# Value projections of the second and third attention group: from two products to one block of 1024 columns by Strassen's method

## The chip, the cores and the metric

The kernel runs on one core of a Trainium2 chip. The metric is the device time of one launch in microseconds. Three runs of the kernel before gave 2731.43 to 2731.93 us, with a median of 2731.71 us; the same kernel with the change is to be timed against it.

## What is computed

Two layers of a post-norm encoder on 256 tokens of 2048 features, all in float32. In each layer `x @ w_in` gives the queries, keys and values of two attentions and two gates; the first attention ("dilated") has three head groups, the second is a windowed attention with grouped queries. Cut to what the change touches:

```python
proj = jnp.einsum('bsd,dc->bsc', x, w_in)              # x: 256 x 2048
qa, ka, va, qb, kb, vb, ga, gb = jnp.split(proj, split_points, axis=-1)
ya = dilated_mixture(qa, ka, va, rel_bias).astype(dt) @ w_pa     # va: 3 groups x 512 columns
yb = windowed_gqa(qb, kb, vb, rel_bias, sink).astype(dt) @ w_pb
merged = jax.nn.sigmoid(ga) * ya + jax.nn.sigmoid(gb) * yb
x = layer_norm(DEEPNORM_ALPHA * x + merged @ w_out, ln1_g, ln1_b)
gate, up = jnp.split(x @ w_up, 2, axis=-1)
x = layer_norm(DEEPNORM_ALPHA * x + (jax.nn.silu(gate) * up) @ w_down, ln2_g, ln2_b)
```

## The kernel before

**Products in three parts.** Every float32 operand of a large product is split into a high part (rounded to the matmul's short float format) and the rest: `split_into` (lines 468 to 470) writes `hi` on ScalarE (ACT) and `lo = src - hi` on VectorE (DVE). A product of two operands is then three matmuls into one PSUM bank: high times high, high times low, low times high (`rows_product`, lines 242 to 247).

**Pieces.** The program is a list of pieces. A piece is one 512 KB weight tile (two tiles of 128 rows by 512 columns, or four by 256) with its load, its split and its matmuls. `run` (line 166) walks the list: before the matmuls of piece m it issues the splits up to piece m + 5 (further ahead round a layer norm, by the `norms` list), and `load_to` issues the loads up to five pieces beyond the split, into seven `raw` buffers on SP's DMA queue. After the matmuls of a piece comes its `post`, and then one entry of the list `soon` or, if that is empty, of `background` (attention steps, bias tables, the affine step of the layer norm), unless the piece is marked `quiet`. What is issued later in this order stands later in the in-order queue of each engine.

**Two ways to do 1024 columns.** `gemm_a` (line 249) multiplies all 256 tokens by 512 columns over 16 tiles of the contraction: 8 pieces, 96 matmuls of 128 x 512, one accumulator (`acc`, two PSUM banks, two buffers). `gemm_s` (line 306) does two such column blocks c1 and c2 together. The 16 contraction tiles are eight pairs. In three of them, marked S in the plan `SCSCSCCC`, it forms seven products instead of eight, so 21 matmuls instead of 24; the other five, C, are done plainly. An S pair takes four pieces (`pair_of_sums`, line 342): the first two load the left and right weight tile, and the four splits of them do on DVE: one full split and the half-width ones `t13`, `b22` (lines 354 to 356), three half-width sums (lines 365 to 368), and two full splits of the sums, `thi` and `tlo`. Its pieces are quiet, as are the C pairs between S pairs. The products of an S pair collect in four single banks (`aux`: q1, q5, q7, q6) and in the four banks of both accumulators (q2, q3 in the first, q4 and the last in the second); the last S pair folds the single banks into two tiles e and f, and the last C pair adds e and f to the accumulators. In three of the C pairs (list `ADDED`) the left tile is split by ACT and a POOL DMA instead of DVE. Before an S pair can run, `sum_rows` (line 439) must have formed the sums of the tokens' side for its pair: four DVE additions, an ACT copy and a DVE subtraction, `sT`.

**The start of a layer.** Here each layer computes the values of the first attention by three `gemm_a` (lines 861 to 863, called VA0, VA1, VA2 below), then the values of the second attention (VB, line 864, 4 pieces), its keys (KB) and its queries. `post_va` (line 834) brings the result to SBUF: for group 0 as a split pair on ACT and DVE, for the others as plain float32, one half on ACT and one on DVE. Pieces are numbered from 0 at the layer's first. In layer 0 the first six pieces also transpose the input (`make`, each with a split `xT` on ACT and DVE), and piece 6 queues the small tables (`setup_small`): the background then holds `turn`, `biases` (a product with the table `hots`) and seven writes of the table `ftab` on SP. In layer 1 the first pieces of VA0 are interleaved with the layer norm before it, and piece 4 adds `late` and twelve background entries of the affine step.

**Where gemm_s is used already.** The gates of column blocks 1 to 3 (`both`, line 916, after one plain `gate(0)`), and 10 of the 11 column blocks of the up product. The first `both` of a layer is called both(1) below; its three `sum_rows` run in the pieces just before it.

## Time and profile before

| | |
|---|---|
| runs, us | 2731.43, 2731.71, 2731.93 |
| profiled execution, us | 2733.02 (span 2731.2) |
| mean granted TensorE clock | 0.997 |
| busy us: TensorE (PE) / weight loads / DVE / ACT / POOL | 2701.2 / 2269.0 / 1894.5 / 1382.3 / 72.8 |
| matmuls / DVE / ACT instructions | 13209 / 2354 / 1679 |
| DMA: MB, mean GB/s | 572.77, 210 |

The span runs from the first to the last instruction; the profiled execution's time is 1.8 us more. A matmul's record in the timeline has a start and a modelled length; neighbouring records overlap, so the distance between starts is what a matmul costs. Three things tell about a place of the program: the start times on PE, the idle time in brackets with what ended it, and what DVE and ACT did at that time.

### The profile page before, as it was taken

What the parts mean: (1) busy time and instruction counts of PE and PEld (TensorE: products, weight loads), DVE (VectorE), ACT (ScalarE), POOL (GpSimd) and SP (SyncE); (2) the same over time, 40 slices, a digit from 0 to 9 for tenths busy, and PEclk for the clock granted to TensorE, in tenths of its full rate; (3) what the DMA queues carried; (4) which work ended last, traced back from release to release, by engine and by line L of the source; (5) the groups of instructions that cost most, each with busy time, mean ns of one, the idle gap of its engine ahead of it and who ended that gap; (6) DMA issues with size and microseconds to landing.
All of it is one profiled execution on the core that took longest, in us unless ns stands there. A gap on an engine that the chain in (4) does not pass through costs nothing. (4 is left out here: it accounts for less than half of the span.)

```text
span 2731.2 us, 35220 instructions
## 1 busy us (share of the span) xinstructions
PE 2701.2 (99%) x13209; PEld 2269.0 (83%) x13209; DVE 1894.5 (69%) x2354; ACT 1382.3 (51%) x1679; POOL 72.8 (3%) x91
## 2 busy tenths in 40 slices
PE   9999999999999999999999999999999999999998
PEld 7888878888888888888888888788888788888887
DVE  5566577766985687577675655777678857875885
ACT  4454455544564465455454544555455545553551
POOL 0000000000000000000000000000000000000000
PEclk9999999999999999999999999999999999999999
DMA  8866567764886687578566565677648757875874
GB/s 260 255 183 182 185 180 241 219 211 139 242 264 208 193 242 232 198 213 255 202 198 180 180 189 174 213 208 231 224 131 249 244 197 206 245 239 177 246 224 132
DMA packets 368991, 572.77 MB, mean 210 GB/s; under 512 B 53536, under 2 KB 150816, under 8 KB 368820
## 3 DMA queue, kind: packets, MB, share of 16 engines
q1 hardware_dynamic: 356788, 528.31, 58.9%
q0 software_dynamic: 11232, 40.90, 8.1%
q8 instruction: 103, 1.69, 0.3%
q10 hardware_dynamic: 800, 1.31, 0.1%
q14 instruction: 68, 0.56, 0.1%
HBM read 522.86 MB, written 6.68 MB: 194 GB/s over the span
## 5 line engine op out<-in xcount | busy, mean ns | idle before, releaser
L470 DVE TENSOR_TENSOR wlo<-raw,whi 128x1024 fp32r<-128x1024 f32 x804 | 951.2, 1220 | 199.0 <-ACT whi L469 155.3
L469 ACT ACTIVATE whi<-raw 128x1024 fp32r<-128x1024 f32 x804 | 815.4, 1052 | 275.3 <-PE acc L247 132.4
L329 PE MATMUL acc<-whi,xT 128*128 128x512 f32 x1118 | 440.3, 394 | 2.9 <-DVE sg L414 2.9
L331 PE MATMUL acc<-whi,xT 128*128 128x512 f32 x1118 | 435.9, 390 | 0.0
L330 PE MATMUL acc<-wlo,xT 128*128 128x512 f32 x1118 | 435.1, 389 | 0.0
L232 PE MATMUL acc<-xT,whi 128*128 128x512 f32 x1088 | 387.1, 399 | 0.0
L201 PE MATMUL acc<-xT,wlo 128*128 128x256 f32 x1088 | 299.7, 281 | 0.0
L469 ACT ACTIVATE thi<-t 128x1024 fp32r<-128x1024 f32 x156 | 165.8, 1063 | 255.4 <-DVE t L367 234.5
L245 PE MATMUL acc<-whi,hT 128*128 128x512 f32 (+1 forms) x752 | 284.3, 378 | 1.9 <-DVE sg L414 1.9
L247 PE MATMUL acc<-whi,hT 128*128 128x512 f32 (+1 forms) x752 | 282.7, 376 | 0.0
L246 PE MATMUL acc<-wlo,hT 128*128 128x512 f32 (+1 forms) x752 | 282.3, 375 | 0.0
L329 PEld LDWEIGHTS acc<-whi,xT 128*128 128x128 f32 x1118 | 209.9, 188 | 48.0 <-issue 4.8
L331 PEld LDWEIGHTS acc<-whi,xT 128*128 128x128 f32 x1118 | 209.8, 188 | 44.5
L330 PEld LDWEIGHTS acc<-wlo,xT 128*128 128x128 f32 x1118 | 210.2, 188 | 42.3
L232 PEld LDWEIGHTS acc<-xT,whi 128*128 128x128 f32 x1088 | 203.0, 188 | 43.3
L201 PEld LDWEIGHTS acc<-xT,wlo 128*128 128x128 f32 x1088 | 205.6, 189 | 2.6
L245 PE MATMUL acc<-whi,xT 128*128 128x512 f32 (+1 forms) x512 | 196.6, 384 | 0.3 <-ACT xT L469 0.3
L247 PE MATMUL acc<-whi,xT 128*128 128x512 f32 (+1 forms) x512 | 193.8, 379 | 0.6 <-DVE xT L470 0.6
L470 DVE TENSOR_TENSOR tlo<-t,thi 128x1024 fp32r<-128x1024 f32 x156 | 190.5, 1221 | 4.0 <-ACT thi L469 0.3
L246 PE MATMUL acc<-wlo,xT 128*128 128x512 f32 (+1 forms) x512 | 193.2, 377 | 0.0
L245 PEld LDWEIGHTS acc<-whi,hT 128*128 128x128 f32 x752 | 141.6, 188 | 28.9 <-issue 3.8
L247 PEld LDWEIGHTS acc<-whi,hT 128*128 128x128 f32 x752 | 141.5, 188 | 26.0
(190 smaller groups left out, 3773.0 us busy)
## 6 DMA issues: line engine op xcount, KB each, us to landing
raw<-in_w_up_dram SPq DMA_DIRECT2D x352, 512.0 KB, 5.2
raw<-in_w_in_dram SPq DMA_DIRECT2D x320, 512.0 KB, 4.7
raw<-in_w_down_dram SPq DMA_DIRECT2D x176, 512.0 KB, 3.9
wlo<-raw POOLq DMA_DIRECT2D x78, 512.0 KB, 6.9
raw<-in_w_out_dram SPq DMA_DIRECT2D x64, 512.0 KB, 4.9
raw<-in_w_pb_dram SPq DMA_DIRECT2D x32, 512.0 KB, 5.5
raw<-in_w_pa_dram SPq DMA_DIRECT2D x16, 512.0 KB, 6.5
bias<-ftab SPq DMA_DIRECT2D x96, 64.0 KB, 2.7
```

The costliest lines, as they stand in the source:

```text
L201: nc.tensor.matmul(st["acc"][:, n, 0:SEQ], lhsT=lo[:, k, n * P:(n + 1) * P], rhs=xs(4 * j + k)[:, 0, :], start=False, stop=False)
L232: nc.tensor.matmul(acc, lhsT=hi[:, k, n * P:(n + 1) * P], rhs=xs(kt).rearrange("p h t -> p (h t)"), start=first and not turn, stop=last)
L245: nc.tensor.matmul(o, lhsT=xk[:, 0, ts], rhs=hi, start=first, stop=False)
L246: nc.tensor.matmul(o, lhsT=xk[:, 0, ts], rhs=lo, start=False, stop=False)
L247: nc.tensor.matmul(o, lhsT=xk[:, 1, ts], rhs=hi, start=False, stop=last)
L329: nc.tensor.matmul(o, lhsT=xk[0], rhs=hi, start=first, stop=False)
L330: nc.tensor.matmul(o, lhsT=xk[0], rhs=lo, start=False, stop=False)
L331: nc.tensor.matmul(o, lhsT=xk[1], rhs=hi, start=False, stop=last)
L469: nc.scalar.activation(hi, src, AF.Copy)
L470: nc.vector.tensor_tensor(out=lo, in0=src, in1=hi.bitcast(F32), op=ALU.subtract)
```

## The change

VA0 stays a `gemm_a`. VA1 and VA2 become one `gemm_s` over columns VA + 512 and VA + 1024 with the plan `SCSCSCCC`; its result tiles are the two plain float32 `va` tiles (`place`). The three `sum_rows` that its S pairs need are put into `soon` at piece 5 of VA0 and so come after pieces 5, 6 and 7 of VA0. The two `post_va` branches for groups 1 and 2 go. The arguments `k0` and `start` and the condition on `quiet` change nothing with this plan. In both layers the two `gemm_a` (16 pieces that each let one background entry go) become 22 pieces, of which 6 do.

```diff
-    def gemm_s(w, c1, c2, xs, sums, post, plan=PLAN):
+    def gemm_s(w, c1, c2, xs, sums, post, plan=PLAN, k0=0, place=None, start=None):
...
-            return w[2 * p * P:(2 * p + 2) * P, c0:c0 + 512].rearrange("(k p) c -> p k c", p=P)
+            return w[(k0 + 2 * p) * P:(k0 + 2 * p + 2) * P, c0:c0 + 512].rearrange("(k p) c -> p k c", p=P)
...
-            st["e"], st["f"] = e, f
+            st["e"], st["f"] = start(e, f) if start else (e, f)
...
-                    out_ = work.tile([P, 2, 512], F32, name="sg", tag="sg", bufs=3)
+                    out_ = st[extra] if start else (place() if place else work.tile([P, 2, 512], F32, name="sg", tag="sg", bufs=3))
...
-                pair_of_blocks(pc_, s_left > 0, i == len(plan) - 1)
+                pair_of_blocks(pc_, 0 < s_left < plan.count("S"), i == len(plan) - 1)
...
         def post_va(acc):
-            if not va:
-                va.append([unit([P, 2, 512], F32R, "va") for _ in range(2)])
-                split_into(*va[0], acc)
-                return
-            v = unit([P, 2, 512], F32, "va")
-            nc.scalar.activation(v[:, 0, :], acc[:, 0, :], AF.Copy)
-            nc.vector.tensor_copy(v[:, 1, :], acc[:, 1, :])
-            va.append(v)
+            va.append([unit([P, 2, 512], F32R, "va") for _ in range(2)])
+            split_into(*va[0], acc)
...
-        for g in range(3):
-            gemm_a(wi, 0, KT, VA + 512 * g, 512, xs, post_va, pre=(pre if g == 0 else None),
-                   turn=(turn if g == 0 else None))
+        vsums = []
+        gemm_a(wi, 0, KT, VA, 512, xs, post_va, pre=pre, turn=turn)
+        before = pieces[-3]["pre"]
+        pieces[-3]["pre"] = lambda: (before() if before else None, soon.extend([
+            lambda i=i: vsums.append(sum_rows(xt[i])) for i in range(SUMS)]))
+        gemm_s(wi, VA + 512, VA + 1024, xs, vsums, lambda a, b: va.extend([a, b]),
+               place=lambda: unit([P, 2, 512], F32, "va"))
         gemm_a(wi, 0, KT, VB, 256, xs, post_vb)
```

What the order of the instructions becomes is shown at three places (the number behind a name tells buffers apart; line numbers of the changed kernel are one higher from line 307 on and two higher from line 431 on).

DVE in layer 0 at the end of VA0, before: `xT_341` is the last input transpose, the `wlo` rows are splits of weight tiles, and `va_413` reads VA0's accumulator `acc_189`.

```order
L470 TENSOR_TENSOR xT_341<-aux_336,xT_341 128x2x256
L470 TENSOR_TENSOR wlo_359<-raw_266,whi_358 128x1024
L508 MEMSET tab_372 128x20
L470 TENSOR_TENSOR wlo_397<-raw_272,whi_396 128x1024
L470 TENSOR_TENSOR va_413<-acc_189,va_412 128x1024
L470 TENSOR_TENSOR wlo_419<-raw_298,whi_418 128x1024
```

The same place in the changed kernel: the rows begin in the first `sum_rows` (`v_357`, `sT_362`), which stands right behind the last `xT`; `tlo_366` is the second split of the first S pair's sums, `wlo_410` that of the first C pair's left tile.

```order
L452 TENSOR_TENSOR v_357<-v_357 128x128
L472 TENSOR_TENSOR sT_362<-v_357,sT_362 128x4x128
L472 TENSOR_TENSOR tlo_366<-t24_329,thi_365 128x1024
L510 MEMSET tab_379 128x20
L446 TENSOR_TENSOR v_401<-xT_172 128x512
L450 TENSOR_TENSOR v_401<-v_401 128x256
L451 TENSOR_TENSOR v_401<-v_401 128x128
L452 TENSOR_TENSOR v_401<-v_401 128x128
L472 TENSOR_TENSOR sT_406<-v_401,sT_406 128x4x128
L472 TENSOR_TENSOR wlo_410<-raw_268,whi_409 128x1024
L472 TENSOR_TENSOR va_426<-acc_189,va_425 128x1024
```

Between the last `xT` and the read of VA0's accumulator there were two weight splits and a memset; now two whole `sum_rows`, two splits and the memset stand there, and the third `sum_rows` follows right behind. In layer 1 the order from the first `sum_rows` on is the same.

PE in layer 0, from the fourth piece of the first S pair: q6 goes to the bank `aux_491`, q4 to `acc_444`, which takes the buffer that VA0's accumulator had.

```order
L330 MATMUL aux_491<-thi_365,sT_362 128x512 [waits PE_49,Activation_49]
L331 MATMUL aux_491<-tlo_366,sT_362 128x512 [waits DVE_49]
L332 MATMUL aux_491<-thi_365,sT_362 128x512
L330 MATMUL acc_444<-thi_365,xT_158 128x512 [waits DVE_49]
L331 MATMUL acc_444<-tlo_366,xT_158 128x512
L332 MATMUL acc_444<-thi_365,xT_158 128x512
L330 MATMUL acc_443<-whi_409,xT_219 128x512 [waits Activation_49]
```

Before, the matmuls behind VA0 went to the other accumulator buffer and did not need VA0's; now the 19th matmul behind VA0 needs it, and waits for DVE.

PE in layer 0 round the product with `hots` (`biases`), before, where it stood behind the second piece of VA1:

```order
L245 MATMUL acc_422<-whi_306,xT_172 128x512
L246 MATMUL acc_422<-wlo_307,xT_172 128x512
L247 MATMUL acc_422<-whi_306,xT_172 128x512
L527 MATMUL aux_457<-hots_378,tab_372 20x448
L527 MATMUL aux_460<-hots_378,tab_372 20x448
```

And in the changed kernel:

```order
L330 MATMUL acc_444<-whi_637,xT_312 128x512
L331 MATMUL acc_444<-wlo_638,xT_312 128x512
L332 MATMUL acc_444<-whi_637,xT_312 128x512
L529 MATMUL aux_743<-hots_385,tab_379 20x448
L529 MATMUL aux_746<-hots_385,tab_379 20x448
```

It now stands between the last two C pairs of the new `gemm_s`; the load of `hots` keeps its place in SP's queue, at piece 6 of VA0. The seven `ftab` writes behind it move back with it: the last one now stands one weight load ahead of the first bias load, which reads `ftab`.

## Rows read from the trace of the kernel before

**Rows 1.** Page, part 1: busy us, share of the span and count by engine.

```profile
PE 2701.2 (99%) x13209; PEld 2269.0 (83%) x13209; DVE 1894.5 (69%) x2354; ACT 1382.3 (51%) x1679; POOL 72.8 (3%) x91
```

**Rows 2.** Timeline of PE: start us, length us, instruction; stage borders, both(1), both(2), two gemm_a pairs.

```profile
378.92 0.39 PE L329 MATMUL aux<-whi,xT 128*128 128x512 f32 x1
...
424.46 0.47 PE L245 MATMUL acc<-whi,oA 128*128 128x512 f32 x1
...
440.90 0.39 PE L329 MATMUL aux<-whi,xT 128*128 128x512 f32 x1
...
483.40 0.47 PE L245 MATMUL acc<-whi,oA 128*128 128x512 f32 x1
...
827.28 0.47 PE L245 MATMUL acc<-whi,hT 128*128 128x512 f32 x1 [1.22 <-DVE sg L414]
...
915.40 0.39 PE L329 MATMUL aux<-whi,xT 128*128 128x512 f32 x1
```

**Rows 3.** Timeline of PE inside both(1); in brackets idle us and what ended it.

```profile
382.34 0.50 PE L330 MATMUL aux<-tlo,sT 128*128 128x512 f32 x1 [0.79 <-DVE tlo L470]
...
385.91 0.50 PE L329 MATMUL acc<-thi,xT 128*128 128x512 f32 x1 [1.43 <-DVE sg L908]
```

**Rows 4.** Timeline of PE in layer 0: VA0's last piece, VA1's first, the hots product.

```profile
34.91 0.39 PE L245 MATMUL acc<-whi,xT 128*128 128x512 f32 x1
...
37.63 0.39 PE L245 MATMUL acc<-whi,xT 128*128 128x512 f32 x1
...
44.94 1.66 PE L527 MATMUL aux<-hots,tab 128*20 128x448 f32 x4 [1.24 <-DMA hots<-const_hot_dram]
```

**Rows 5.** Timeline of DVE at both(1): last sum_rows (first row), half sums, splits.

```profile
375.98 0.69 DVE L444 TENSOR_TENSOR v<-xT 128x512 f32<-128x512 f32 x1
...
379.14 0.68 DVE L367 TENSOR_TENSOR t<-raw 128x512 f32<-128x512 f32 x1
...
381.07 2.51 DVE L470 TENSOR_TENSOR tlo<-t,thi 128x1024 fp32r<-128x1024 f32 x2
```

**Rows 6.** Timeline of ACT there: the copy of sum_rows, weight copies.

```profile
377.87 0.63 ACT L469 ACTIVATE sT<-v 128x512 fp32r<-128x512 f32 x1 [3.21 <-DVE v L450]
...
382.23 2.94 ACT L469 ACTIVATE whi<-raw 128x1024 fp32r<-128x1024 f32 x3
```

**Rows 7.** Timeline of DVE in layer 0, end of VA0.

```profile
29.43 2.35 DVE L470 TENSOR_TENSOR wlo<-raw,whi 128x1024 fp32r<-128x1024 f32 x2
31.70 0.68 DVE L470 TENSOR_TENSOR xT<-aux,xT 128x512 fp32r<-128x512 f32 x1
...
33.43 0.68 DVE L470 TENSOR_TENSOR xT<-aux,xT 128x512 fp32r<-128x512 f32 x1
...
38.89 1.22 DVE L470 TENSOR_TENSOR va<-acc,va 128x1024 fp32r<-128x1024 f32 x1 [2.50 <-ACT va L469]
```

**Rows 8.** Timeline of DVE in layer 1, VA0: weight splits, splits behind late, va.

```profile
1378.35 4.62 DVE L470 TENSOR_TENSOR wlo<-raw,whi 128x1024 fp32r<-128x1024 f32 x4
...
1385.01 3.49 DVE L470 TENSOR_TENSOR wlo<-raw,whi 128x1024 fp32r<-128x1024 f32 x3
1394.17 1.23 DVE L470 TENSOR_TENSOR va<-acc,va 128x1024 fp32r<-128x1024 f32 x1 [5.67 <-ACT va L469]
```

**Rows 9.** Timeline of PE in layer 1: first matmul of VA1.

```profile
1392.87 0.39 PE L245 MATMUL acc<-whi,xT 128*128 128x512 f32 x1
```

**Rows 10.** Source line 150 (the POOL DMA of 512 KB): shortest, median, longest us to landing.

```profile
DMA to landing us min/median/max: 4.5/6.9/8.0
```

**Rows 11.** Timeline of PE at the start; the last row a window: busy by engine, granted clock, DMA.

```profile
9.00 0.30 PE L549 MATMUL aux<-ident,res 128*128 128x128 f32 x1 [2.21 <-DMA res<-in_x_dram]
...
11.18 0.63 PE L245 MATMUL acc<-whi,xT 128*128 128x512 f32 x1
...
14.17 0.42 PE L246 MATMUL acc<-wlo,xT 128*128 128x512 f32 x1
...
13.00:14.00 1.00, 1.00 (x4) 0.81 (x3) 1.00 (x2) 0.28 (x1) 0.00 (x0) 0.50 1.06 236
```

More of the change, by code (lines that the diff above doesn't have):

```diff
@@ L333, in rows @@
         def rows(kt, t):
-            return [xs(kt)[:, i, t * P:(t + 1) * P] for i in (0, 1)]
+            return [xs(k0 + kt)[:, i, t * P:(t + 1) * P] for i in (0, 1)]
         def total(p, i):
@@ L429, in gemm_s @@
             if step == "S":
+                assert ps < SUMS
                 s_left -= 1
```

## The prediction

> **What bounds the kernel now.** I read the page's busy times first. TensorE is busy 2701.2 of 2731.2 us [rows 1], so only fewer matmuls or fewer waits on it can shorten the kernel. The record of a matmul overstates its cost: the last piece of VA0 has 12 matmuls between 34.91 and 37.63 [rows 4], so one costs 0.2267 us. I then looked for the waits of TensorE in its timeline. There are few, and two kinds matter here. In both(1) the first S pair waits twice for DVE, 0.79 us for the split of a sum and 1.43 us until DVE has read the accumulator of the product before [rows 3]. As a stage both(1) takes 45.54 us from its first matmul to the next product's first; both(2), with the same instructions, takes 42.50 [rows 2]. So a `gemm_s` that begins while DVE is behind costs 3.04 us more than one that begins with DVE ahead. The other wait is the 1.24 us for the table `hots` in layer 0 [rows 4]. The question is how far DVE is behind where the new `gemm_s` begins, and I read the timelines of DVE and ACT there.
>
> **Fewer matmuls.** Each layer loses 3 S pairs times 3 matmuls, 9 times 0.2267 = 2.04 us. Measured as stages, two pairs of `gemm_a` take 88.12 us, 44.06 a pair, against 42.50 for both(2) [rows 2], a difference of 1.56; but the `gemm_s` stage carries the eight transposes of one block and the other eight over two pairs, so 1.56 is too little. I take 1.9, near the upper end, and 3.8 us for two layers; 3.1 and 4.1 are the ends.
>
> **The wait for hots.** The product with `hots` moves 159 matmuls into the `gemm_s`, 36 us behind its start, while its load stays where it was. The 1.24 us [rows 4] go; the matmuls themselves stay. What is late next there is nothing on TensorE.
>
> **What DVE must do in the way, layer 0.** The durations: a weight split on DVE 4.62/4 = 1.15 [rows 8], `tlo` 2.51/2 = 1.25, a half-width operation 1.93/3 = 0.64 in a row of three, and a whole `sum_rows` 379.14 - 375.98 = 3.16, including the ACT copy in its middle [rows 5]. On ACT the copy `sT` takes 0.63 and starts 1.9 after the sum did, and a copy of a weight tile 2.94/3 = 0.98 [rows 6]. With them I walk along the queues in the order shown above, from the place where both kernels still agree.
>
> - At 29.43 DVE did two weight splits in 2.35 [rows 7]. Now it does one and the two half-width operations `t13`, `b22`: about the same. `xT` of the seventh transpose runs at 31.8 instead of 31.70.
> - Then come three half sums (1.93) and a `tlo` (1.25) in the place of one split. The last `xT` runs from 35.5 to 36.2 instead of from 33.43. The last piece of VA0 starts at 34.91 and needs it with its third matmul, at 35.36: 0.85 us of waiting, and VA0 ends at 38.5 instead of 37.63.
> - The first `sum_rows` lasts to 39.3; the second `tlo` waits for its ACT copy behind `sT` (38.6 to 39.6) and ends at 40.8; the second `sum_rows` ends at 43.9. ACT then copies C1's left tile to 44.3 and VA0's result to 45.3; DVE splits the tile to 45.4 and reads VA0's accumulator to 46.6. Before, DVE did that at 38.89 and had been idle for 2.50 us [rows 7].
> - TensorE has 18 matmuls before q4 needs that accumulator: 38.5 + 4.1 = 42.6. It waits 4.0 us.
> - The third `sum_rows` ends at 49.8, with the copy of C1's right tile behind it on ACT at 50.1 and its split on DVE at 51.3. TensorE wants it at 46.6 + 15 matmuls + 0.25 = 50.3: 1.0 us.
> - DVE then owes S2 a split, two half operations, three half sums and a `tlo`, 5.5 us, to 56.8; TensorE comes to it at 56.0: 0.8 us. The left tile of C2 is split by the POOL DMA: ACT is done with it at 52.6, the DMA lands 6.9 later [rows 10], at 59.5, and TensorE needs it at 59.3: 0.2. From here DVE has one split to do in a C pair of 24 matmuls (5.4 us) and comes ahead again.
>
> Together 6.85 us in layer 0.
>
> **The same in layer 1.** Four splits stood at 1378.35 [rows 8]; now three and two half operations, no longer. `late` ends at 1385.1 as before. Three half sums, `tlo`, the first sum and the second `tlo` end at 1393.0, the second sum at 1396.2, C1's left split at 1397.7, the read of the accumulator at 1398.9. Here 5.67 us in which DVE was idle before [rows 8] have taken up part of it. VA0 ends at 1392.87 [rows 9], q4 is due 4.1 later at 1396.95: 1.95 us of waiting. C1's right tile is ready at 1403.6 and wanted at 1402.55: 1.05. S2's `tlo` is ready at 1409.1 and wanted at 1408.35: 0.75. No other wait follows; 3.75 us in all.
>
> **Costed at nothing.** The entry into VB behind the `gemm_s`: the products that follow both(1) and both(2) start without idle time [rows 2]; the one behind the up stage waited 1.22 us [rows 2], which bounds it from above, per layer. Evacuating VA1 and VA2: DVE and ACT work off the path, before as after. The twelve affine entries of layer 1 and the `ftab` writes of layer 0 come later, behind fewer pieces. The first bias load must now wait on SP for a table write issued just ahead of it, and the weight loads behind it wait too; a 512 KB transfer lands 4.5 to 8.0 us after its issue [rows 10], and splits run five pieces of 2.7 us ahead of the matmuls, which covers it. Without that cover it is one wait of up to 8.0 us, once. The weight bytes are the same.
>
> **The clock.** At the start TensorE idles 2.21 us, and soon after that the granted clock is 0.50, the 1.2 GHz level: seven steps between 11.18 and 14.17 take 0.427 us each [rows 11]. The idle 1.24 and 1.43 us [rows 3, 4] are shorter, and the mean clock is 0.997. The 4.0 us of waiting in layer 0 are longer than any of these in the middle of the kernel. The Trainium skill, "TensorE: Matmul & The Clock Gate", section "Why this matters for your kernels", says that idle gaps between bursts of matmuls put the array back to half rate; by that rule the sum is 1.4 us higher, which rows of this case give as its price below. I leave a fall of the clock out of the sum, because the start's idle time came behind small transposes and not behind a full stream of matmuls, and price it as a rival.
>
> **The sum.** -3.8 - 1.24 + 6.85 + 3.75 = +5.6 us. Against the profiled execution's 2733.02 us that is 2738.6. The median of the runs is 1.3 us lower than that execution, so I predict 2737.3 us. A measurement of this kernel can tell about 0.2%, 5.5 us, from no change: the forecast stands on that edge.
>
> **Rivals.**
>
> *The clock falls in layer 0's wait.* For it: the row above. Against it: the wait is broken by nothing, but it is a single one. It decides if TensorE stands idle longer than at the start. Price: seven matmuls at 0.427 instead of 0.2267, 1.4 us; 2738.7 us, slower.
>
> *DVE is not as late as my walk.* If the three `sum_rows` find gaps that I do not see, the hand-over costs what it costs in both(1), 3.04 us per layer [rows 2]. For it: the same instructions are there, and the three sums stand just before the S pair too. Against it: in both(1) only the third sum stands in the way, here the second and third do, with the read of a whole accumulator on both ACT and DVE between. -3.8 - 1.24 + 6.08 = +1.0: 2732.7 us, not slower. It decides if DVE has read VA0's accumulator by 44.0 in layer 0, 1.43 us after q4 is due at 42.6.
>
> *The cover holds.* No wait at either hand-over, as in both(2) [rows 2]. -5.0 us: 2726.7. Against it: between 29 and 43 DVE in layer 0 has two sums (6.3 us) and the half sums and `tlo` for one split (2.0) more to do, and was idle there for only 2.50 [rows 7]. Even this is under 0.2%.
>
> *The POOL DMA is late.* C2's left tile is due when its DMA lands at the median. At the longest landing, 8.0 instead of 6.9 [rows 10], each layer waits 1.1 us more: +2.2, 2739.5 us, slower.
>
> That the change does not do what it says is excluded: the order shows 18 matmuls fewer and the seven products where they belong.
>
> **How the numbers follow.** Forecast 0.45 (its own range 2735.0 to 2739.5, from half a microsecond on each of the walk's larger steps in either direction), the clock 0.15, both(1)'s hand-over 0.25, no wait 0.07, POOL 0.08. Slower by over 0.2% (above 2737.2): a little over half of the forecast, 0.25, with the clock and POOL 0.48. Within 0.2%: the rest of the forecast 0.20, both(1) 0.25, nearly all of no wait: 0.51. Faster by over 0.2%: 0.01, since the most that can be gained is 5.0 us. The range 2731.8 to 2740.5 holds all but the no-wait case and the tails: below, both(1)'s case less 0.9 us; above, the clock or a late POOL DMA with another microsecond.
>
> **What would show it.** In the profile of the changed kernel: 18 matmuls fewer; no idle time at the product with `hots`; in layer 0 an idle time of 3 to 4 us before q4's first matmul, released by DVE's `va`, and in layer 1 one of 1.5 to 2; smaller ones behind `wlo` in C1's right piece and behind `tlo` in S2; both(1) and the later stages as they were. I am wrong if DVE's `va` of layer 0 ends before 44, if the new stage takes under 44 us in layer 1 (42.5 less its transposes and with the waits it is 45.5), or if waits show up in VB, in KB or at the bias loads.

## The result and the profile after

Six runs of the changed kernel give 2743.62 to 2749.55 us, median 2744.98; six of the kernel before, timed with them, 2731.19 to 2732.82, median 2731.82. The ratio is 1.0051 (95% interval 1.0039 to 1.0063): slower by 13 us, where I predicted 2737.3 and a range up to 2740.5. The profiled execution took 2743.7 us, its span is 2741.9, so the spans differ by 10.7 us, and those are explained below; the other 2.5 are the scatter of the runs round their profiles. Of the 7.7 us between forecast and median, 5.1 are in the profile (10.7 where I had 5.6), and the rest is that scatter.

The page's first part, against [rows 1]: 18 matmuls fewer, and TensorE is busy longer all the same.

```profile
PE 2702.4 (99%) x13191; PEld 2267.9 (83%) x13191; DVE 1933.7 (71%) x2426; ACT 1400.7 (51%) x1701; POOL 78.2 (3%) x97
```

TensorE's timeline (start us, length us, instruction, in brackets idle us and what ended it), against [rows 4, 9]: layer 0 up to the end of the KB, QB, QA and KA products, then layer 1's start.

```profile
35.38 0.50 PE L247 MATMUL acc<-whi,xT 128*128 128x512 f32 x1 [0.65 <-DVE xT L472]
...
37.82 0.39 PE L330 MATMUL aux<-whi,xT 128*128 128x512 f32 x1
...
41.67 0.39 PE L332 MATMUL aux<-thi,sT 128*128 128x512 f32 x1
45.70 0.80 PE L330 MATMUL acc<-thi,xT 128*128 128x512 f32 x1 [3.63 <-DVE va L472]
...
48.79 0.40 PE L331 MATMUL acc<-wlo,xT 128*128 128x512 f32 x1
...
98.50 0.40 PE L232 MATMUL acc<-xT,whi 128*128 128x512 f32 x1
...
319.60 0.39 PE L245 MATMUL acc<-whi,xT 128*128 128x512 f32 x1
...
1401.88 0.39 PE L330 MATMUL aux<-whi,xT 128*128 128x512 f32 x1
...
1407.70 0.50 PE L330 MATMUL acc<-thi,xT 128*128 128x512 f32 x1 [1.57 <-DVE va L472]
...
1412.29 0.50 PE L331 MATMUL acc<-wlo,xT 128*128 128x512 f32 x1 [0.66 <-DVE wlo L472]
...
1417.69 0.50 PE L331 MATMUL aux<-tlo,sT 128*128 128x512 f32 x1 [0.34 <-DVE tlo L472]
...
1458.49 0.40 PE L232 MATMUL acc<-xT,whi 128*128 128x512 f32 x1
```

The same borders in the kernel before are, beside [rows 4, 9], these; 1447.90 is the start of KB in layer 1.

```profile
96.28 0.40 PE L232 MATMUL acc<-xT,whi 128*128 128x512 f32 x1
...
310.49 0.39 PE L245 MATMUL acc<-whi,xT 128*128 128x512 f32 x1
...
1447.90 0.40 PE L232 MATMUL acc<-xT,whi 128*128 128x512 f32 x1
```

| stretch, us | before | after | difference | my sum |
|---|---|---|---|---|
| layer 0 up to KB's first matmul | 96.28 | 98.50 | +2.2 | +3.7 |
| layer 0, KB to the last KA ("the W stage" below) | 214.21 | 221.10 | +6.9 | 0 |
| layer 1, VA0's end to KB | 55.03 | 56.61 | +1.6 | +1.85 |
| everything else | | | 0.0 | 0 |

The two stretches with the hand-overs lost 3.8 us, where I had 5.6. The first of them also holds the start of the launch: the first product began at 10.24 before and at 10.96 after. The miss is the second line, a stage whose own instructions the change does not touch. There SP's queue and DVE tell the story. First SP before (the last of the seven table writes, the weight loads behind it, the first bias loads), then SP after (first and last write, the one weight load behind it, the first bias loads).

```profile
93.50 0.44 SPq L531 DMA_DIRECT2D ftab<-fb  x1
94.03 20.77 SPq L135 DMA_DIRECT2D raw<-in_w_in_dram  x12
114.86 7.43 SPq L540 DMA_DIRECT2D bias<-ftab  x8
```

```profile
81.28 0.32 SPq L533 DMA_DIRECT2D ftab<-fb  x1
...
124.42 0.44 SPq L533 DMA_DIRECT2D ftab<-fb  x1
124.94 5.31 SPq L135 DMA_DIRECT2D raw<-in_w_in_dram  x1
132.27 5.25 SPq L542 DMA_DIRECT2D bias<-ftab  x8
```

DVE and TensorE of the changed kernel behind that, and five windows (from and to, length, busy us of PE, weight loads, DVE, ACT and POOL, granted clock, DMA share, GB/s), two behind the wait for `va` and three behind the wait for `p`:

```profile
135.40 0.48 DVE L785 CUSTOM_DVE_ANT_0 p<-aux,bias,sink_bc 128x256 f32<-128x256 f32 x1 [8.96 <-DMA bias<-ftab]
```

```profile
139.63 0.59 PE L801 MATMUL aux<-ident,p 128*128 128x128 f32 x3 [3.03 <-DVE p L794]
...
148.27 0.39 PE L476 MATMUL aux<-pt,vb 128*128 128x256 f32 x1 [0.34 <-ACT pt L471]
149.65 0.39 PE L477 MATMUL aux<-pt,vb 128*128 128x256 f32 x1 [0.99 <-DVE pt L472]
```

```profile
46.00:47.00 1.00, 1.00 (x3) 0.81 (x3) 0.93 (x3) 0.00 (x0) 0.00 (x0) 0.50 0.85 289
47.00:48.00 1.00, 1.00 (x4) 0.71 (x3) 0.32 (x2) 0.61 (x2) 0.00 (x0) 0.50 1.02 389
...
140.00:142.00 2.00, 2.00 (x11) 1.72 (x11) 1.97 (x6) 0.00 (x0) 0.00 (x0) 0.71 1.05 343
142.00:144.00 2.00, 2.00 (x8) 1.71 (x7) 0.59 (x4) 1.96 (x6) 0.00 (x0) 0.50 1.09 358
144.00:146.00 2.00, 2.00 (x14) 1.82 (x13) 2.00 (x4) 0.75 (x2) 0.00 (x0) 0.93 0.75 241
```

Before, twelve weight loads stood between the last write and the first reader of the table. Now one does; the reader is issued 7.85 us behind the write. For 5.31 of them SP was busy issuing the weight load between the two, and for 1.9 it waited until the write had landed. DVE, which works in order, then stands 8.96 us before the first softmax, and TensorE, which meets the transposes of `p` in its own order, 3.03 us, with the clock at 0.50 behind it and 1.33 us more of waits for `pt`. At granted clocks of 0.71, 0.50 and 0.93 three windows of 2 us lose 1.7 us. Idle time and clock together come to 6.1 of the 6.9 us; the brackets leave out the rest, since a record's length (0.39 us) overstates a matmul (0.23).

### The profile page after: what moved, and what is told of

The parts are those of the page before. It is cut to its first block, busy times and chain, and to the rows that moved or that the text cites. A ratio compares the mean times of both kernels' runs of the same rounds, so it can differ in the third digit from the quotient of the medians.

```text
span 2741.9 us, 35325 instructions
## 1 busy us (share of the span) xinstructions
PE 2702.4 (99%) x13191; PEld 2267.9 (83%) x13191; DVE 1933.7 (71%) x2426; ACT 1400.7 (51%) x1701; POOL 78.2 (3%) x97
## 5 line engine op out<-in xcount | busy, mean ns | idle before, releaser
L472 DVE TENSOR_TENSOR wlo<-raw,whi 128x1024 fp32r<-128x1024 f32 x792 | 936.8, 1220 | 175.3 <-ACT whi L471 132.4
L471 ACT ACTIVATE whi<-raw 128x1024 fp32r<-128x1024 f32 x792 | 804.0, 1051 | 255.0 <-PE acc L247 132.6
L330 PE MATMUL acc<-whi,xT 128*128 128x512 f32 x1204 | 474.5, 394 | 3.1 <-DVE sg L415 3.1
L332 PE MATMUL acc<-whi,xT 128*128 128x512 f32 x1204 | 469.7, 390 | 0.0
L331 PE MATMUL acc<-wlo,xT 128*128 128x512 f32 x1204 | 468.9, 389 | 0.7 <-DVE wlo L472 0.7
L471 ACT ACTIVATE thi<-t 128x1024 fp32r<-128x1024 f32 x168 | 178.5, 1062 | 266.8 <-DVE t L368 243.6
L330 PEld LDWEIGHTS acc<-whi,xT 128*128 128x128 f32 x1204 | 226.3, 188 | 52.5 <-issue 5.8
L332 PEld LDWEIGHTS acc<-whi,xT 128*128 128x128 f32 x1204 | 226.1, 188 | 47.9
L331 PEld LDWEIGHTS acc<-wlo,xT 128*128 128x128 f32 x1204 | 226.5, 188 | 47.0 <-DVE wlo L472 1.1
L472 DVE TENSOR_TENSOR tlo<-t,thi 128x1024 fp32r<-128x1024 f32 x168 | 205.2, 1222 | 4.3 <-ACT thi L471 0.5
L246 PEld LDWEIGHTS acc<-wlo,hT 128*128 128x128 f32 x752 | 141.6, 188 | 25.3
L245 PE MATMUL acc<-whi,xT 128*128 128x512 f32 (+1 forms) x384 | 146.6, 382 | 0.0
L247 PE MATMUL acc<-whi,xT 128*128 128x512 f32 (+1 forms) x384 | 143.9, 375 | 0.6 <-DVE xT L472 0.6
```

Of the source, the lines that this page charges most:

```text
L245: nc.tensor.matmul(o, lhsT=xk[:, 0, ts], rhs=hi, start=first, stop=False)
L246: nc.tensor.matmul(o, lhsT=xk[:, 0, ts], rhs=lo, start=False, stop=False)
L247: nc.tensor.matmul(o, lhsT=xk[:, 1, ts], rhs=hi, start=False, stop=last)
L330: nc.tensor.matmul(o, lhsT=xk[0], rhs=hi, start=first, stop=False)
L331: nc.tensor.matmul(o, lhsT=xk[0], rhs=lo, start=False, stop=False)
L332: nc.tensor.matmul(o, lhsT=xk[1], rhs=hi, start=False, stop=last)
```

## The experiments

My first theory (T): the loss is the first bias load's wait for the last write, which now stands right ahead of it. Rivals named along the way: the writes use up the lead of the weights (D), they block SP's queue (Q), or they cost DMA time whoever issues them (B, S, W); and, for the rest, that DVE's lateness (H) or the clock decides. This table collects what the sections below refer to, from each run's profile (issue times on SP, us) and its median. Each ratio is to runs of the kernel before that were timed with that run (their medians lie between 2731.4 and 2732.7).

| run | last ftab write | first bias load | W stage | median, us | ratio to before, interval |
|---|---|---|---|---|---|
| before | 93.50 | 114.86 | 214.21 | 2731.82 | |
| the change | 124.42 | 132.27 | 221.10 | 2744.98 | 1.0039 to 1.0063 |
| e1_tables_early | 117.31 | 131.90 | 229.48 | 2751.15 | 1.0053 to 1.0083 |
| e2_before_tables_late | 120.87 | 129.19 | 220.10 | 2738.42 | 1.0012 to 1.0030 |
| e3_layer1_only | 94.00 | 114.90 | 214.22 | 2733.44 | 0.9994 to 1.0013 |
| e4_one_sum | 121.31 | 129.70 | 219.47 | 2741.68 | 1.0020 to 1.0045 |
| e6_bias_later | 123.69 | 133.26 | 218.60 | 2740.3 | 1.0019 to 1.0041 |
| e7_vb_first | 123.31 | 131.61 | 226.33 | 2745.03 | 1.0031 to 1.0056 |
| e8_bias_later_warm | 124.88 | 134.69 | 218.17 | 2739.43 | 1.0015 to 1.0033 |
| e9_tables_on_pool | on POOL, 82.9 to 90.5 | 145.54 | 239.23 | 2762.35 | 1.0092 to 1.0123 |
| e10_vb_first_tables_spread | 111.11 | 134.57 | 214.52 | 2751.67 | 1.0055 to 1.0081 |
| e11_wide_writes | 126.92 | 134.53 | 220.58 | 2745.2 | 1.0037 to 1.0062 |
| e12_vb_first_wide | 109.52 | 121.74 | 219.65 | 2734.14 | 0.9999 to 1.0017 |
| e13_before_wide | 86.62 | 113.66 | 214.21 | 2732.78 | 0.9993 to 1.0011 |
| e14_vb_first_keys_first | 125.74 | 154.20 | 214.27 | 2729.06 | 0.9983 to 1.0001 |
| e15_keys_first | 123.87 | 157.86 | 214.40 | 2737.52 | 1.0013 to 1.0032 |
| e16_before_keys_first | 91.63 | 157.19 | 214.40 | 2732.68 | 0.9995 to 1.0012 |

**e2_before_tables_late.** The old kernel with twelve more empty background entries ahead of the table steps, so that the tables come late.

```diff
-        background.extend([lambda: None, lambda: None, turn, biases])
+        background.extend([lambda: None] * 14 + [turn, biases])
```

> The kernel before, with one edit: twelve empty background entries ahead of the table steps of layer 0, so that the last ftab write stands one weight load ahead of the first bias load, as in the change; no Strassen in the value projections. Theory T: the same chain appears without the change's products: DVE waits about 8 us for bias, TensorE about 3 us with a fall of the clock after it, the stage grows by about 6.9 us, the wait for hots (1.24 us) goes: about 5.6 us above before, near 2737.4. Rival D predicts the same sign but no wait released by the bias load. Rival H: within 1.5 us of before.

2738.42 us, and the W stage 220.10. The old kernel loses 5.9 us in that stage without a single Strassen piece in V. DVE waits for the bias load and TensorE for `p`, as in the change; a window (columns as above) shows the clock behind that wait:

```profile
132.49 0.48 DVE L783 CUSTOM_DVE_ANT_0 p<-aux,bias,sink_bc 128x256 f32<-128x256 f32 x1 [8.14 <-DMA bias<-ftab]
...
136.47 0.70 PE L799 MATMUL aux<-ident,p 128*128 128x128 f32 x4 [1.97 <-DVE p L792]
```

```profile
138.00:140.00 2.00, 1.99 (x12) 1.49 (x10) 0.81 (x5) 1.12 (x5) 0.00 (x0) 1.00 1.06 355
```

TensorE has four waits there, 1.97 and 1.01 us for `p`, 0.60 and 0.99 for `pt`, and its clock stays at 1.00 throughout the stage. So the order of the tables alone makes a loss of nearly this size, and the half clock that the change shows there is not needed for it.

**e1_tables_early.** The changed kernel without the empty entries between the writes.

```diff
-                background.extend([lambda: None, lambda d=d: nc.sync.dma_start(
+                background.extend([lambda d=d: nc.sync.dma_start(
```

> The change, with one edit: the seven writes of ftab stand in seven consecutive background entries instead of every second one, so the last is issued seven pieces before the first bias load instead of one weight load before it. Theory T (the first bias load of layer 0 waits on SP for the last ftab write, DVE stands behind it, TensorE waits for DVE and then runs at half clock): DVE's 8.96 us wait for bias and TensorE's 3.03 us wait at the transposes of p go, the stage of the KB, QB and QA/KA products in layer 0 falls from 221.1 us to about 214.2, time 6.9 us under the change, near 2738. Rival D (the tables crowd the weight loads wherever they come after the gemm_s): the stage stays above 218 us. Rival H (the hand-over into the gemm_s is nearly all of the loss): the time stays within 2 us of the change.

A miss, and a useful one: 2751.15, 6 us slower than the change. The writes did end earlier, but the first bias load did not come earlier, and TensorE ran out of weights:

```profile
135.23 0.58 PE L476 MATMUL aux<-parts 128*128 128x256 f32 x1 [12.08 <-ACT parts L471]
```

ACT had waited for `raw` there; each weight load behind a write took SP 2.9 to 5.1 us to issue. A write is not a short entry in a queue, it is work.

**e3_layer1_only** and **e4_one_sum** take the hand-over apart. e3 keeps the three `gemm_a` in layer 0. e4 forms only the first of the three sums and uses it for all three S pairs: sums 2 and 3 are left out.

```diff
+        if l == 1:
...
+        else:
+            for g in range(3):
+                gemm_a(wi, 0, KT, VA + 512 * g, 512, xs, post_va, pre=(pre if g == 0 else None),
+                       turn=(turn if g == 0 else None))
```

```diff
-            lambda i=i: vsums.append(sum_rows(xt[i])) for i in range(SUMS)]))
+            lambda: vsums.extend([sum_rows(xt[0])] * SUMS)]))
```

> The change in layer 1 alone; layer 0 is that of the kernel before. Theory T with the hand-over as walked: layer 0 takes the time of before, layer 1 is 1.6 us longer from VA1's start to VB's end (56.6 instead of 55.0), so 1.6 us above before, 2733.4. Rival (layer 1 gains, all loss is in layer 0): 1.9 us under before. With H: 3 us or more above.

2733.44, 0.9 us above the kernel before, which the noise covers. Its profile shows the loss: from VA0's end to KB layer 1 takes 56.56 us (1393.22 to 1449.78) instead of 55.03, as the third row of the table of stretches says. The loss in the W stage does not occur.

> The change with only the first sum_rows done and its result used for all three S pairs, so the sums of the second and third pair of token tiles are left out. Theory of the DVE queue: in layer 0 VA0's accumulator is read 3.1 us earlier, q4 waits 0.5 us or less instead of 3.63, no half clock follows there (1.3 us), the waits in C1 and S2 go: the gemm_s stage falls from 49.1 to about 43.5 us; in layer 1 from 45.0 to about 42.3. The wait for bias stays. Together about 8 us under the change, near 2737. Rival (q4 waits for ACT's copy of the accumulator or for something other than the sums): the waits stay as they are, time within 1.5 us of the change.

2741.68. In layer 1 the new stage fell from 45.02 to 42.86 us, so sums 2 and 3 are what makes DVE late there. In layer 0 the wait for `va` fell from 3.63 to 0.19 us, but the stage grew from 49.09 to 52.59: TensorE came sooner to C2's left tile, whose POOL DMA was issued at 49.01 and landed 9.8 us later.

```profile
58.81 0.80 PE L331 MATMUL acc<-wlo,xT 128*128 128x512 f32 x1 [3.88 <-DMA wlo<-raw]
```

That is my fourth rival, at a longer landing than its 8.0 us; in the change itself the wait for `va` had hidden it.

**e6_bias_later** and **e8_bias_later_warm.** e6 delays the first reader by four pieces; e8 also fills TensorE's wait in layer 0.

```diff
-        background.extend(order)
+        background.extend([lambda: None] * (4 if layer == 0 and chunk == 0 else 0) + order)
```

```diff
                 product("q6", total(p, 2), hi[:, 0, :], lo[:, 0, :])
+                for _ in range(warm if p == 0 else 0):
+                    nc.tensor.matmul(st["q6"][:, 0:SEQ], lhsT=zeros[:, 0:P], rhs=zeros, start=False, stop=False)
```

> The change, with four empty background entries put ahead of the first attend_b of layer 0, so that the first bias load is issued four pieces (14 us) later and the last ftab write, which landed 7.85 us after its issue in the changed kernel, is done by then. Theory T (the 6.9 us that layer 0's KB/QB/QA/KA stage lost are the wait of SP for the last ftab write, and of DVE, TensorE and its clock behind it): the stage is 214.2 us again, no wait of TensorE for p, and the kernel is at 2745.0 - 6.9 = 2738.1 us. Theory D (the seven ftab writes between weight loads have used up the weight lead, as they did when they came at every piece, where TensorE waited 12.08 us for weights): the stage stays above 218 us with waits for weights or for splits, and the time above 2742.

218.60: only 2.5 of the 6.9 us are gone, between the two theories. Four pieces later in the program was 1 us later on SP (133.26 instead of 132.27), since the five weight loads in between, behind the last write, took SP 8.93 us. DVE still stood before `p`:

```profile
142.90 0.48 DVE L785 CUSTOM_DVE_ANT_0 p<-aux,bias,sink_bc 128x256 f32<-128x256 f32 x1 [5.67 <-DMA bias<-ftab]
```

TensorE's wait for `p` shrank to 0.18 us. What is left there are two waits for `pt`, 0.60 and 1.00 us, and a fall of the clock behind them, which takes another 1.7 us (granted 0.82, 0.50 and 0.83 in the windows of 2 us from 156 to 162):

```profile
158.00:160.00 2.00, 2.00 (x8) 1.71 (x8) 2.00 (x3) 0.50 (x1) 0.00 (x0) 0.50 0.83 212
```

> As e6_bias_later, and in layer 0, ahead of q4's first matmul, 32 matmuls of a zero tile (bfloat16, 256 columns) into q6's bank, which add nothing to it and last about as long as TensorE waits there (3.63 us). If the idle time is what lets the clock fall, the granted clock stays 1.00 between 46 and 49 us, q4's matmuls and those behind follow at 0.227 instead of 0.427 us, and the stage is about 1.3 us shorter than in e6_bias_later: 2736.8 us if that one is at 2738.1. If the clock falls for another reason, or the fill delays q4, it is the same as e6_bias_later or longer.

The clock did what was expected, the time did not. With the fill it stays at 1.00:

```profile
42.94 3.67 PE L391 MATMUL aux<-zeros 128*128 128x256 bf16 x32
46.75 0.50 PE L330 MATMUL acc<-thi,xT 128*128 128x512 f32 x1
...
51.33 0.50 PE L331 MATMUL acc<-wlo,xT 128*128 128x512 f32 x1 [0.62 <-DVE wlo L474]
...
56.74 0.50 PE L331 MATMUL aux<-tlo,sT 128*128 128x512 f32 x1 [0.35 <-DVE tlo L474]
```

```profile
47.00:48.00 1.00, 1.00 (x5) 0.80 (x5) 0.93 (x3) 0.00 (x0) 0.00 (x0) 1.00 0.82 211
```

But the `gemm_s` stage takes 49.12 us in both e6 and e8. At full clock TensorE meets the waits for `wlo` and `tlo` that I had predicted; at half clock it comes too late to meet them. The 1.5 us of half clock (in the change, seven steps take 3.09 us, below) cost nothing there; I read this as DVE setting the pace.

**e9_tables_on_pool** and **e11_wide_writes** ask what a write costs. In e9 the issue moves, in e11 the pieces grow to 4 KB:

```diff
-                background.extend([lambda: None, lambda d=d: nc.sync.dma_start(
+                background.extend([lambda: None, lambda d=d: nc.gpsimd.dma_start(
```

```diff
+        def write(d, fb):
+            wide = unit([N_HEADS, 8, P], F32, "wide")
+            nc.scalar.activation(wide, fb[:, d][:, None, :].to_broadcast([N_HEADS, 8, P]), AF.Copy)
+            nc.sync.dma_start(ftab[:, d].rearrange("h (r a) n -> h r (a n)", a=8),
+                              wide.rearrange("h a n -> h (a n)")[:, None, :].to_broadcast([N_HEADS, 8, 8 * P]))
...
-                background.extend([lambda: None, lambda d=d: nc.sync.dma_start(
-                    ftab[:, d], fb[:, d][:, None, :].to_broadcast([N_HEADS, 64, P]))])
+                background.extend([lambda: None, lambda d=d: write(d, fb)])
```

> The change, with the seven ftab writes of layer 0 issued on POOL's DMA queue instead of SP's, at the same place of the program. In the changed kernel the issue of the weight load that stands behind an ftab write takes SP 3 to 6 us (5.31 us behind the last one) where others take 0.4, and each write with its two weight loads takes 7.1 us against the 6.7 us in which TensorE consumes two tiles. Theory Q (SP's queue is what the writes block: they stood there ahead of the bias loads and the weights, and the stage begins without the lead that it had): SP is free, the writes run beside the weights, the bias load finds ftab written, and the KB/QB/QA/KA stage of layer 0 is at 214.2 to 215.5 us instead of 221.1: 2738 to 2739.5 us in all. Theory B (it is the DMA engines' bandwidth that the 4.6 MB of writes take, whoever issues them): POOL, which waits for nothing, issues all seven in a burst, the weights behind it land late, and TensorE waits for splits at the end of the gemm_s or in VB: 2742 us or more.

Theory B, by far: 2762.35. SP was free and it did not help. The DMA issues between 83 and 128 us (size of one, median us from issue to landing), and two windows, one from before the burst and one in it:

```profile
ftab<-fb POOLq DMA_DIRECT2D x7, 640.0 KB, 40.0
raw<-in_w_in_dram SPq DMA_DIRECT2D x6, 512.0 KB, 39.2
```

```profile
70.00:80.00 10.00, 10.00 (x47) 8.20 (x46) 7.61 (x10) 5.31 (x5) 0.00 (x0) 1.00 1.02 319
...
100.00:110.00 10.00, 10.00 (x58) 8.65 (x58) 3.14 (x3) 2.61 (x3) 0.00 (x0) 1.00 1.01 131
```

With the DMA engines as busy, 131 GB/s went through instead of 319, and seven writes, issued within 8 us, kept the weights waiting for 40. The Trainium skill, "DMA: Bandwidth & Descriptors", section "Issuing engines are not separate DMA queues", says that transfers run on the same DMA engines whoever issues them; this run agrees.

> The change, where each ftab write takes its rows from a tile that ACT has filled with eight copies of the 128 values (20 partitions x 1024, one activation of about 1 us more per write), so that it consists of 160 pieces of 4 KB instead of 1280 of 512 bytes; bytes and place are the same. In e9_tables_on_pool the DMA engines were all busy from 83 to 128 us and moved only 130 GB/s, against 340 where weights alone run: a write of 655 KB costs 5 to 6 us of all DMA engines. Theory S (it is the small pieces): a write costs 2 to 3 us, a weight load behind it is issued in about 1 us instead of 3 to 6, the weights keep their lead, and the KB/QB/QA/KA stage of layer 0 is 214.2 to 216 us instead of 221.1: 2738 to 2740 us in all. Rival W (the cost hangs on the bytes or on the twenty partitions that are read): no better than the change, 2744 to 2746.

Half of it. The loads behind a write were issued in 1.0 to 3.4 us for two instead of 6.7, but the stage is 220.58: the last write was still on its way 7.6 us after its issue (126.92 to 134.53), and SP waited for it 6.7 us. So the small pieces hold up the loads behind them, and the time to landing is not theirs. The stage itself tells less: the copies into `wide` stand in ACT's order, SP waited 23.1 us in all for four of them, and the last write was issued 2.5 us later than in the change. Whether wide writes that are issued in time would save the stage is not shown by this run.

**e13_before_wide**, the control: the same `write` in the kernel before.

> Control: the kernel before, with the wide ftab writes alone. There the writes stand at 46 to 94 us, ahead of KB, and no wait of TensorE stands behind them: the same as before under every theory, 2731 to 2732.5 us, if anything shorter by the wait for hots (no: that load does not change). If it is faster by over 0.2%, the writes cost something in the kernel before as well, and e12's gain is not the change's.

2732.78, no difference.

**e7_vb_first, e10_vb_first_tables_spread, e12_vb_first_wide** look for a better order. All have VB between VA0 and the new `gemm_s`:

```diff
+        gemm_a(wi, 0, KT, VB, 256, xs, post_vb)
         gemm_s(wi, VA + 512, VA + 1024, xs, vsums, lambda a, b: va.extend([a, b]),
                place=lambda: unit([P, 2, 512], F32, "va"))
-        gemm_a(wi, 0, KT, VB, 256, xs, post_vb)
```

> The change, with VB's product (4 pieces, 11.6 us of TensorE) moved between VA0 and the new gemm_s in both layers. Theory H (the hand-over waits come from DVE being 3 to 4 us late with sums 1 and 2 right behind VA0): DVE has VB's 11.6 us to catch up with 4 weight splits of 1.15 us, so xT keeps 0.65 us in layer 0 but q4, wlo and tlo wait together under 1 us in each layer, and no clock falls there; VB's four pieces also let four background entries go earlier, so the last ftab write comes about 14 us earlier and the bias load does not wait: 2731.8 - 3.8 - 1.2 + 1.5 = 2728.3 us. Rival R (DVE's debt is only moved: VB's pieces are as dense for DVE as VA's, and the read of VB's accumulator takes the place of that of VA0's): a wait for an accumulator of 1.4 us as in both(1) in each layer and the small ones behind it, 3 us a layer: 2731 to 2733 us.

Nearly right on DVE in layer 0, wrong on the total. The wait for `va` is gone (two of 1.23 and 0.26 us, behind `biases` and `turn`, come in its place) and KB starts at 92.63 instead of 98.50. But the writes kept their times on SP (VB's four entries come earlier and later entries fill the same places, so "14 us earlier" was miscounted), and TensorE, 5.9 us earlier, waited 8.37 us for `p` instead of 3.03. In layer 1 the affine step, with a wait of 4.32 us for its vectors on DVE, now stood ahead of the last additions:

```profile
138.97 1.11 PE L801 MATMUL aux<-ident,p 128*128 128x128 f32 x4 [8.37 <-DVE p L794]
...
1453.84 0.47 PE L330 MATMUL acc<-whi,xT 128*128 128x512 f32 x1 [2.06 <-DVE va L415]
```

```diff
-        background.extend([lambda: None, lambda: None, turn, biases])
+        background.extend([turn, lambda: None, biases])
...
-            background.extend([lambda: None] * 5)
+            background.extend([lambda: None] * (9 if late2 else 5))
...
+            for i in range(7):
+                pieces[s0 + 3 * i]["pre"] = lambda i=i: tables[i]()
```

(the first part and the second, which is layer 1's, are in e12 and e14 too; `tables` holds the seven writes).

> A version that is to beat both kernels: VB between VA0 and gemm_s as in e7_vb_first, and three shifts. In layer 0 turn and biases come after VB's first and third piece instead of its third and fourth, so that the four aux banks of the first S pair need not wait for them (0.26 and 1.23 us in e7_vb_first); the seven ftab writes are issued ahead of every third piece of the gemm_s (about every 7 to 8 us from 48 us on, as before the change) instead of behind its end; in layer 1 the affine step starts four entries later, so that DVE's 4.32 us for its vectors do not stand ahead of the gemm_s's last additions (2.06 and 0.65 us in e7_vb_first). If the failed step is where the writes stand (SP's stream of loads is behind TensorE when attention starts), layer 0's KB/QB/QA/KA stage is 214.2 us, the start of layer 0 up to KB about 4.4 us shorter than before the change and that of layer 1 about 1.6: 2731.8 - 6 = 2726 us, faster than before by 0.2%. If writes ahead of the gemm_s's pieces starve it of weights, TensorE waits for splits or POOL's DMA inside it, and the time is 2730 or more.

Its second case: 2751.67. The W stage is clean (214.52) and layer 1 up to the last KA 2.0 us shorter than before, but inside layer 0's `gemm_s` the writes starved the weights; the longest wait:

```profile
111.73 0.76 PE L331 MATMUL acc<-whi,xT 128*128 128x512 f32 x1 [6.30 <-DVE va L416]
```

> A version that is to beat both kernels: VB between VA0 and gemm_s, the wide ftab writes of e11_wide_writes, at every second background entry behind the gemm_s's last S pair and done two pieces earlier than before, turn and biases behind VB's first and third piece, the affine step of layer 1 four entries later. In e10_vb_first_tables_spread layer 0's attention had no waits once the writes were over, and layer 1's start was 2.0 us shorter than before the change; what was lost was 6 to 30 us inside the gemm_s of layer 0, where the small writes held up its weights. If theory S holds: layer 0 up to KB 4.4 us shorter than before the change, KB to KA as before, layer 1 2.0 shorter: 2732.0 - 6.4 = 2725.6 us. If the writes are as slow as they were: above 2735.

2734.14, 11 us better than the change and 0.08% above before. Layer 0 up to KB is 3.9 us shorter and layer 1 up to the last KA 2.0, but two wide writes issued back to back ended 12.2 us after the second:

```profile
107.63 0.50 SPq L527 DMA_DIRECT2D ftab<-wide  x1
...
109.52 0.82 SPq L527 DMA_DIRECT2D ftab<-wide  x1
...
121.74 5.26 SPq L550 DMA_DIRECT2D bias<-ftab  x8
```

The two, with the three weight loads that SP issued among them, took 14.1 us. So a write takes 6 to 7 us, one after the other, and seven take 45 to 50; this is an estimate from e12, from e9 (seven in some 45 us of full DMA engines) and from the change (81.28 to 132.27), and in all of these weight loads shared the engines.

**e15_keys_first, e16_before_keys_first, e14_vb_first_keys_first** settle it. In layer 0 the first pair of QA and KA (24 pieces) goes ahead of KB and QB; nothing is done to the writes.

```diff
...
+        if l:
+            windowed()
         for pair in range(2):
+            if pair and not l:
+                windowed()
```

(`windowed` holds the products KB and QB as they were.)

> The change, with only the order of layer 0's products behind VB changed: the first pair of QA and KA ahead of KB and QB. The seven ftab writes keep their places and durations, and the first bias load comes 80 us later. Theory L (the writes are a job of 45 to 50 us of DMA time that now begins 35 us later and ends after the first attention wants its table): no wait for p, no half clock there, the stage takes 214.2 instead of 221.1 us: 2738.1 us. Theory D (it is the weight lead that the writes use up, whatever stands behind them): TensorE waits for weights or splits before 140 us all the same, the stage takes over 217: 2741 to 2745.

Theory L: 2737.52, and no wait in the W stage. Its borders:

```profile
96.96 0.40 PE L232 MATMUL acc<-xT,whi 128*128 128x512 f32 x1
...
311.36 0.40 PE L245 MATMUL acc<-whi,xT 128*128 128x512 f32 x1
```

The writes run at the same times as in the change (79.74 to 123.87) and cost TensorE nothing, because the table is read 34 us after the last. It is also 0.2 us from my forecast of 2737.3, which had left just this loss out. That closeness is in part luck: the stretches that my sum covers lost 3.8 us instead of 5.6, and e15's median lies 2.0 us above its own profiled execution (2735.57).

> Control: the kernel before, with the same order of layer 0's products. Its writes are done at 100 us under either order, so only the reordering itself is measured: 2731.8 us, within 0.1%; up to 4 us more if attention steps are left over for the merge.

2732.68, no difference: the reordering by itself is worth nothing.

> A version that is to beat both kernels: VB between VA0 and gemm_s with turn and biases after VB's first and third piece and the affine step of layer 1 four entries later (as in e12_vb_first_wide), the ftab writes as in the change, and in layer 0 the first pair of QA and KA (24 pieces, 80 us) ahead of KB and QB, so that the first bias load stands 24 pieces behind the gemm_s instead of 8. In e12 the start of layer 0 was 3.9 us and that of layer 1 2.1 us shorter than before the change, and the KB/QB/QA/KA stage of layer 0 lost 5.4. If that loss is nothing but the deadline of the writes, it goes: 2731.8 - 6.0 = 2725.8 us, faster than before by 0.2%. If the writes still empty the weight lead while they run, or the attention steps, now later, pile up in front of the merge, 2729 to 2733.

2729.06 us, the fastest of all, 16 us under the change and 0.08% under before (interval -0.17% to +0.01%): probably faster than before, but not shown. Layer 0's start is 82.27 us long (10.84 to 93.11) where before took 86.04, the stretch from the down product of layer 0 to the last KA of layer 1 361.48 (363.32). In its profile the only new wait on the way is the first row below; in layer 1's up stage 2.0 us were lost behind `sg`, which e12's profile, with the same instructions there, does not show.

```profile
55.50 0.50 PE L330 MATMUL acc<-thi,xT 128*128 128x512 f32 x1 [0.60 <-DVE vb L472]
...
93.11 0.47 PE L232 MATMUL acc<-xT,whi 128*128 128x512 f32 x1
```

## Why the prediction was right and wrong

- **Fewer matmuls, the wait for hots.** Right: 18 matmuls fewer, and no wait at the product with `hots`.
- **The walk in layer 0.** The large term held: q4 starts 4.03 us behind its predecessor (41.67 to 45.70), 3.80 more than a step of 0.23, where I had 4.0; `xT` waits 0.65 by its bracket and 0.80 by the starts (0.85). The 1.0 for C1 and 0.8 for S2 did not show, and in their place came the half clock that I had as a rival: the seven steps from 45.70 to 48.79 take 3.09 us instead of 1.59. In e8 the clock stays up and the small waits come instead, in the same total: what the clock takes, the waits give back. From the new stage's first matmul to KB the loss is 2.03 us (60.68 against 58.65), where I had 2.86 without `xT`. What `xT` cost the launch can't be told: the first product began between 9.2 and 11.7 us in the profiles of all the runs.
- **The clock.** I left its fall out because one wait behind a full stream of matmuls was not seen to bring it. It fell behind 3.63 idle us, and again behind 3.03 in the W stage; e8 fills the first of these gaps with matmuls, and there it does not fall. The Trainium skill, "TensorE: Matmul & The Clock Gate", section "Why this matters for your kernels", has idle gaps between bursts bring half rate; the windows at 46 and 142 us agree. How long the idle time must be these runs do not tell: in e2 the clock stayed at 1.00 behind 1.97 and 1.01 us and behind 0.60 and 0.99, and in e6 it fell behind 0.60 and 1.00. In layer 0's `gemm_s` it cost nothing. In the W stage it was not tried apart from the waits, but e2 loses 5.9 us there at full clock, where the change loses 6.9.
- **The walk in layer 1.** By the starts, less a step, TensorE waits 1.73 us (1405.74 to 1407.70), 0.83 (1411.23 to 1412.29) and 0.50 (1416.96 to 1417.69), 3.06 in all, where I had 1.95, 1.05 and 0.75, 3.75 in all. The stretch lost 1.6 instead of 1.85, so the rest of it gained 1.5, where I had put 1.9 for the fewer matmuls. e4 shows that the waits come from sums 2 and 3.
- **The step that failed** stands under "Costed at nothing": "The first bias load must now wait on SP for a table write issued just ahead of it ... splits run five pieces of 2.7 us ahead of the matmuls, which covers it." I looked for cover for the weight loads behind the waiting bias load, and that cover was there. I did not follow its reader: the softmax on DVE, which stands in front of every later split, and the transposes of `p`, which stand in TensorE's order and which no split ahead can hide. And I priced the write as one transfer of 4.5 to 8.0 us. Taken singly that holds, since the reader was issued 7.85 us behind it; but it is the last of a row of seven that takes 45 to 50 us and keeps SP busy, and that began at 81.28 instead of 46.53. Begun 35 us later, the row used up the 21 us that had lain between the last write's issue and its reader (93.50 to 114.86). e2 shows that this alone costs the old kernel 5.9 us in that stage, e15 that the change without it stands at 2737.5. My text priced the case without cover at up to 8.0 us, but left it out of the sum and out of the rivals; 6.9 were lost. Waits at the bias loads were named there as a sign that I am wrong, and that sign came.
- **The order of the rivals.** POOL's DMA, at 0.08, was one step from being right: e4 takes the wait for `va` away and gets 3.88 us for that DMA instead. That the hand-over would cost what both(1) does was wrong in layer 0 (3.63 us at the accumulator against 1.43).
- What stays open: why a write of 640 KB takes 6 to 7 us (the size of its pieces is not the reason, e11), why e2 loses 1 us less than the change in the W stage, what idle time brings the clock down, and whether e14 is faster than the kernel before.

## What to carry to other kernels

When a change takes places from a list of background work, everything behind it moves, so follow each moved transfer to its reader, on every engine on which the reader stands in line, and not only to the transfers behind it. A row of writes to memory is a job with a length and a deadline: give it its own line in the sum, with when it starts, how long it runs, and who reads it first. Where one engine sets the pace, a wait or a slow clock on another that you remove comes back as the next wait; price them as one.

## What the hardware showed unexpectedly

- A table write of 640 KB from 20 partitions to memory, spread over 1280 pieces of 512 bytes, takes 6 to 7 us beside weight loads and holds up the issue of the weight load behind it: that takes 3 to 6 us, where others take 0.4. Seven at once brought the DMA rate from 319 to 131 GB/s. With pieces of 4 KB the issue behind it is quick again, and the write as slow.
- Delaying an instruction by four pieces in the program delayed it by 1 us on SP: the queue was that far behind its own program.
- In the changed kernel's stretch of writes a weight load of 512 KB landed a median of 8.4 us after its issue, against 5.0 over all of them:

```profile
raw<-in_w_in_dram SPq DMA_DIRECT2D x13, 512.0 KB, 8.4
```
